# A block gathered three ahead, units of experts in another order, and a last norm with its subtraction on ScalarE

## The chip, the cores and the metric

The kernel runs on one core of a Trainium2 chip. The metric is the time of one execution on the device in microseconds (us). The engines are named as the profile names them: PE is TensorE's matmul side and PEld its weight load, DVE is VectorE, ACT is ScalarE, POOL is GpSimd, SP is SyncE, which issues most DMAs.

## The reference

One decoder block over 512 tokens of width 1024: an adaptive norm, a mixer (a Mamba-2 scan beside a short convolution, joined by gates), a residual and norm, then a mixture of experts, then a residual and norm. Everything is f32. What the change touches is the mixture of experts and the last norm:

```
scores = sigmoid(h @ router_w)             # 512 tokens x 64 experts
e_idx  = top 8 experts of each token, out of its best 4 of 8 groups
gate   = 2.5 * scores[e_idx] / sum(scores[e_idx])
routed[t] = sum over the 8 experts e of t: gate * (silu(h[t] @ w_gate[e]) * (h[t] @ w_up[e])) @ w_down[e]
shared = (silu(h @ sh_gate) * (h @ sh_up)) @ sh_down
x = layer_norm(ALPHA * x + g2 * (routed + shared)) * ln2_g + ln2_b
```

w_gate and w_up are 1024 x 256 and w_down is 256 x 1024 for each expert, so an expert has 3 MiB of weights, read once.

## The kernel before

**Blocks and units.** The experts are ranked by how many tokens they have, and the ranks have fixed capacities (320, 192, 160, 128, 96, 64 and 32 tokens). A block is 128 rows of tokens that belong to one expert or to a few (two of 64, or 96 + 32, or four of 32). Blocks are put together into units of two to six experts by the string ORDER (line 41): each letter is a kind. x is the first rank (3 blocks, 2 experts), y a rank of 192 tokens with a 64 one (2 blocks, 2 experts), z a rank of 160 with a 96 one (2 blocks, 2 experts), f one expert of 128, a a 96 with a 32, p two of 64, q four of 32 (1 block each). So ya has 3 blocks and 4 experts, ap 2 blocks and 4 experts, za 3 and 4, qy 3 and 6, qff 3 and 6, faa 3 and 5. A unit of two experts with fixed names (the static one, 1 block) runs before them. There are 41 blocks in all.

**What happens to a block.** `slots` (line 1108 on) finds its tokens: VectorE compares positions with a ramp (`oh`), TensorE multiplies that one-hot matrix by the tokens' numbers and gates (L1124, tile ps_st), VectorE adds the parts (`red`, L1127), makes an integer list (`idx`, L1129), and GpSimd's queue starts an indirect DMA (L1132) that gathers 128 rows of h from DRAM into one of NXG = 3 buffers `xgs`, used in turn (the profile calls it pg<-h_d,idx). Later `xsteps` transposes the block on TensorE: two halves of four 128x128 transposes (L150, ps_tr<-ident,pg), each half into one of two PSUM banks, from which ScalarE (and for blocks of one expert VectorE, L158 and L160) copies it to `xt`.

**A unit's order on TensorE.** From line 1436 on, for the rest of the units, TensorE's instructions keep the order in which the program is written. In `unit(n)`, TensorE first does the gate and up products of unit n (ps_pj<-...,xt), then, step by step between each other: the transposes of the activations, the combine products of the unit before (L1188 and L1189, which put the weighted rows back to their tokens; VectorE adds them to the residual, L1194), and the transposes of the next unit's blocks by `xs_steps`. That function transposes block i and then calls `need_s(i + NXG)`, which runs `slots` for every block below i + 3. The combine products are used up before the last block of a unit with three blocks is transposed, so its eight transposes stand alone in the order. I call this stretch the transposing stretch. Then come the down products (ps_y<-...,wkr), whose results VectorE weights (L1165) and splits.

**Weights.** SyncE's queue loads the weights in pieces of 1 MiB (lines 869 and 872) into a ring of seven pairs of pages and two more; a piece may be issued up to AHEAD = 10 pieces before its use and when the ring's buffer has been released by the matmuls that read it. An expert has two pieces of gate and up halves and one of down.

**The last norm.** `finish` works on four tiles of 128 tokens. `square` makes the mean and the sum of squares (L1483, ScalarE L1484), `root` the inverse deviation (ScalarE L1488, VectorE L1489), `scale` the result. ENG3 (line 46) says how: for tile 0 ("PP") ScalarE subtracts and scales (L1491, L1492) and GpSimd multiplies by ln2_g (L1501) and adds ln2_b (L1502). For tiles 1 to 3 ("VV") VectorE does it in two instructions with two tensors each (L1497, L1498). Then SyncE writes the tile out (L1503).

Of the kernel before, what the change touches and what calls it, by code (L numbers as in the profile page):

```python
# [8 lines left out]
F32 = mybir.dt.float32  # L9
# [9 lines left out]
T, D, P = 512, 1024, 128  # L19
# [18 lines left out]
NXG = 3  # L38


ORDER = "x qy ya ap za qff ya ap za faa ya ap za faa p"
AHEAD = 10
NDEF = 2
FORD = "q0 r0 s0 q1 r1 s1 q2 r2 s2 q3 r3 s3"
NADA = 3
ENG3 = ("PP", "VV", "VV", "VV")
NWK = 5
AD = "VVVV"
NCV = 4
# [14 lines left out]
def block_kernel(ctx: ExitStack, tc: tile.TileContext, a, out, dbg=None):  # L64
    nc = tc.nc
    dbg = dbg or {}
    V, S, PE, GP, SY = nc.vector, nc.scalar, nc.tensor, nc.gpsimd, nc.sync
# [22 lines left out]
    def bank(tag, bufs, dt=F32):  # L90
        return ps.tile([P, 512], dt, name="ps_" + tag, tag=tag, bufs=bufs)
# [16 lines left out]
    def page(shape, dt=F32, pool=None):  # L108
        n = 1
        for q in shape:  # L110
            n *= q
        assert n == 1024
        if pool or not pw:
            return (pool or pa).tile([P, *shape], dt, name="pg", tag="pg")
        if not halves:
            t = pair([2, 1024], dt)
            halves.extend((t[:, 1], t[:, 0]))
        return halves.pop()
# [618 lines left out]
    rt = ctx.enter_context(tc.tile_pool(name="rt", bufs=1))  # L737
# [159 lines left out]
    def xsteps(src_ap, dst=None, whole=False):  # L897

        hi, lo = dst or [None if whole and i else hold.tile([P, KD, P], F32 if whole else FR, name="xt", tag="hm", bufs=8)
                         for i in range(2)]  # L900
        sv = src_ap.rearrange("p (d k) -> p k d", k=KD)

        def steps():
            for q in range(2):
                tp = bank("tr", 2)
                for k in range(4):
                    transpose(tp[:, k * P:(k + 1) * P], sv[:, 4 * q + k, :])
                tv = tp.rearrange("p (k n) -> p k n", k=4)
                sl_ = slice(4 * q, 4 * q + 4)
                if whole:  # L910
                    S.activation(hi[:, sl_, :], tv, AF.Copy)
                else:
                    split_to(hi[:, sl_, :], lo[:, sl_, :], tv)
                yield

        return (hi, lo), steps()
# [191 lines left out]
    def slots(*parts):  # L1108


        oh = rt.tile([P, NT, P], BF, name="oh", bufs=2)
        w = min(n for _, n, _ in parts)
        i, tiles = 0, []
        for v, n, pays in parts:
            m = len(pays)
            V.tensor_tensor(oh[:, :, i:i + n * m].rearrange("p t (q s) -> p t q s", q=m),
                            iota1[:, None, None, :n].to_broadcast([P, NT, m, n]),
                            v[:, :, :, None].to_broadcast([P, NT, m, n]), op=OP.is_equal)
            i += n * m
            tiles += [p_ for p_ in pays for _ in range(n // w)]  # L1120
        ip = bank("st", 1)
        for t in range(NT):
            for q, p_ in enumerate(tiles):
                PE.matmul(ip[w * q:w * q + w, :6], oh[:, t, w * q:w * q + w], p_[:, t],  # L1124
                          start=(t == 0), stop=(t == NT - 1), tile_position=(0, w * q) if w < P else None)
        red = rt.tile([P, 2], F32, name="red", bufs=8)
        V.tensor_reduce(red, ip[:, :6].rearrange("p (a b) -> p a b", b=3), axis=AX.X, op=OP.add)  # L1127
        idx = rt.tile([P, 1], I32, name="idx", bufs=4)
        V.tensor_scalar(idx, red[:, 0:1], NOTOK, None, op0=OP.add)  # L1129
        xg = xgs[nblk[0] % NXG]  # L1130
        nblk[0] += 1
        GP.indirect_dma_start(out=xg, out_offset=None, in_=h2_d[:, :],  # L1132
                              in_offset=bass.IndirectOffsetOnAxis(ap=idx, axis=0),
                              bounds_check=T - 1, oob_is_err=False)
        return xg, red
# [101 lines left out]
    def static_slots(u):  # L1237
        return slots((pg[:, :, 0, u[0]:u[-1] + 1], P // len(u), [pays[:, :, e, :] for e in u]))
# [61 lines left out]
    def seg(r, n, m=1, v=None):  # L1300
        return (posp if v is None else v)[:, :, r:r + m], n, [pay[:, :, r + i, :] for i in range(m)]

    def second(r):
        pc = rt.tile([P, NT, 1], F32, name="pc")
        V.tensor_scalar(pc, posp[:, :, r:r + 1], 128.0, None, op0=OP.subtract)
        return slots((pc, P, [pay[:, :, r, :]]))
# [20 lines left out]
    for k, n in (("p", 64), ("q", 32)):  # L1327
        m = 128 // n
        for r in of[n][::m]:
            kinds[k].append((tuple(range(r, r + m)),  # L1330
                             [(tuple(range(m)), lambda r=r, n=n, m=m: slots(seg(r, n, m)))]))
    for ks in ORDER.split():

# [18 lines left out]
    def need_s(n):  # L1352
        while len(sl) < min(n, len(allb)):
            sl.append(allb[len(sl)][1]())

    def xs_steps(n):
        while len(xs) < min(n, len(allb)):
            i = len(xs)
            need_s(i + 1)
            r, g = xsteps(sl[i][0], None, len(allb[i][0]) > 1)  # L1360
            xs.append(r)
            yield from g
            need_s(i + NXG)

    def need_x(n):
        drain(xs_steps(n))
# [109 lines left out]
    def finish():  # L1476

        os_, st = {}, {}

        def square(t):  # L1480
            os_[t] = page([D])
            st[t] = const.tile([P, 4], F32, name="fst", bufs=4)
            V.tensor_scalar(st[t][:, 0:1], rsum[:, t, 0:1], rsum[:, t, 1:2], -1.0 / D, op0=OP.add, op1=OP.mult)  # L1483
            S.activation(os_[t], ra[t], AF.Square, bias=st[t][:, 0:1], scale=1.0, accum_out=st[t][:, 1:2])  # L1484

        def root(t):
            nmu, ss, rs, nb = (st[t][:, i:i + 1] for i in range(4))
            S.activation(rs, ss, AF.Sqrt, bias=epsc, scale=1.0 / D)  # L1488
            V.reciprocal(rs, rs)  # L1489
            if ENG3[t] != "VV":  # L1490
                V.tensor_tensor(nb, nmu, rs, op=OP.mult)  # L1491
                S.activation(os_[t], ra[t], AF.Identity, bias=nb, scale=rs)  # L1492

        def scale(t):
            o, nmu, rs = os_[t], st[t][:, 0:1], st[t][:, 2:3]
            if ENG3[t] == "VV":
                V.scalar_tensor_tensor(o, ra[t], nmu, ln2g, op0=OP.add, op1=OP.mult)  # L1497
                V.scalar_tensor_tensor(o, o, rs, ln2b, op0=OP.mult, op1=OP.add)  # L1498
            else:
                e1, e2 = ({"V": V, "P": GP}[e] for e in ENG3[t])  # L1500
                e1.tensor_tensor(o, o, ln2g, op=OP.mult)  # L1501
                e2.tensor_tensor(o, o, ln2b, op=OP.add)  # L1502
            SY.dma_start(out[0, t * P:(t + 1) * P, :], o)  # L1503

        for c in FORD.split():
            {"q": square, "r": root, "s": scale}[c[0]](int(c[1]))
# [35 lines left out]
```

## Time and profile before

| | |
|---|---|
| median of 3 runs | 1628.57 us (1625.51 to 1630.03) |
| the profiled execution | 1629.32 us |
| its span in the trace | 1627.5 us |
| TensorE busy | 1496.8 us, 92% |
| VectorE busy | 974.6 us, 60% |
| ScalarE busy | 645.4 us, 40% |
| GpSimd busy | 230.3 us, 14% |

Times inside the trace count from the start of the span. The 1.8 us by which the execution is longer than its span lie outside the trace. The units of experts run from about 850 to 1600 us, the last norm from 1605 to the end. Idle time of an engine matters only where the next work waits for that engine; the trace gives for each idle stretch what ended it.

### The profile page before, as it was taken

Reading aid. Unit: us, or ns where it says so; the run is one execution under the profiler, and the core shown is the slowest. Engines: PE = TensorE matmul, PEld = TensorE weight load, DVE = VectorE, ACT = ScalarE, POOL = GpSimd, SP = SyncE. Lnnn points to the kernel's source line nnn. Section 1 sums busy time; section 2 is a strip of 40 time slices with the busy share of each in tenths; the row PEclk is TensorE's granted clock in tenths of the full one; section 3 lists DMA queues with packets and bytes.
Section 4 is the critical chain, followed back from the end, with each engine's and each line's share of the span. In section 5 each row is a group of like instructions: output and inputs, shape, how many; then the busy total and the mean of one; then the engine's idle time right before and its main releaser. Section 6 shows DMA issues by size and latency. Waiting matters only on the chain.

```text
span 1627.5 us, 22863 instructions
## 1 busy us (share of the span) xinstructions
PE 1496.8 (92%) x8253; PEld 1018.3 (63%) x8253; DVE 974.6 (60%) x1810; ACT 645.4 (40%) x925; POOL 230.3 (14%) x232
## 2 busy tenths in 40 slices
PE   6999999999999999999978899988889988998893
PEld 3688777787777877887755544545544555554452
DVE  4558778667858556536786535545554554444456
ACT  2456575655634545334542213222341232222222
POOL 0011110111012457300135000000010000000001
PEclk9999999999999999999999999999999999999997
DMA  9653432533441667536227677877988878877671
GB/s 277 170 154 88 113 70 83 147 85 97 117 100 39 203 202 217 167 91 212 108 77 289 234 283 286 305 297 302 386 303 304 309 255 358 317 301 297 253 302 53
DMA packets 194504, 335.67 MB, mean 206 GB/s; under 512 B 13428, under 2 KB 136660, under 8 KB 186196
## 3 DMA queue, kind: packets, MB, share of 16 engines
q1 hardware_dynamic: 183300, 303.73, 53.9%
q0 software_dynamic: 11088, 30.45, 7.3%
q8 instruction: 66, 1.08, 0.3%
q14 instruction: 50, 0.41, 0.1%
HBM read 334.58 MB, written 4.28 MB: 208 GB/s over the span
## 4 chain that ended last, share of the span: by engine, by line
PE 68%; DMA 12%; DVE 8%; issue 6%; ACT 3%; POOL 1%; SPq 1%; DVEq 0%; ACTq 0%; POOLq 0%
PE ps_pj L153 12%; PE ps_pj L154 12%; PE ps_pj L155 12%; PE ps_pj L950 6%; DMA pr<-in_w_up_dram 5%; PE ps_y L950 5%; PE ps_y L1188 4%; PE ps_y L1189 4%; PE ps_tr L150 4%; DMA pg<-h_d,idx 4%; DMA pg<-in_w_ada_dram 2%; DVE wl L160 2%; PE ps_y L153 1%; PE ps_y L155 1%; PE ps_y L154 1%
## 5 line engine op out<-in xcount | busy, mean ns | idle before, releaser
L153 PE MATMUL ps_pj<-hm,wh 128*128 128x512 f32 x680 | 276.3, 407 | 2.0 <-ACT wh L158 2.0
L155 PE MATMUL ps_pj<-hm,wl 128*128 128x512 f32 x680 | 267.4, 394 | 6.2 <-DVE wl L160 6.2
L154 PE MATMUL ps_pj<-hm,wh 128*128 128x512 f32 x680 | 267.4, 393 | 0.0
L160 DVE TENSOR_TENSOR wl<-pg,wh 128x1024 fp32r<-128x1024 f32 (+1 forms) x129 | 157.1, 1224 | 116.9 <-ACT wh L158 116.7
L950 PE MATMUL ps_pj<-pr,xt 128*32 128x512 f32 (+1 forms) x1472 | 212.2, 604 | 9.7 <-DMA pr<-in_w_up_dram 9.7
L158 ACT ACTIVATE wh<-pg 128x1024 fp32r<-128x1024 f32 (+1 forms) x135 | 127.5, 952 | 136.4 <-PE ps_pj L154 104.6
L950 PEld LDWEIGHTS ps_pj<-pr,xt 128*32 128x32 f32 (+1 forms) x1472 | 62.0, 117 | 150.1 <-issue 139.7
L153 PEld LDWEIGHTS ps_pj<-hm,wh 128*128 128x128 f32 x680 | 128.9, 190 | 36.7 <-issue 6.0
L155 PEld LDWEIGHTS ps_pj<-hm,wl 128*128 128x128 f32 x680 | 128.5, 189 | 36.7 <-DVE wl L160 8.8
L154 PEld LDWEIGHTS ps_pj<-hm,wh 128*128 128x128 f32 x680 | 128.5, 189 | 28.9 <-issue 3.4
L160 DVE TENSOR_TENSOR wl<-pr,wh 128x1024 fp32r<-128x1024 f32 x72 | 86.9, 1220 | 96.6 <-ACT wh L158 96.0
L1132 POOL DMA_INDIRECT pg<-h_d,idx x41 | 48.1, 1174 | 597.2 <-PE ps_y L1189 163.6
L1194 DVE TENSOR_TENSOR res<-res,ps_y 128x512 f32<-128x512 f32 x120 | 82.2, 686 | 75.3 <-PE ps_y L1189 73.7
L150 PE MATMUL ps_tr<-ident,pg 128*128 128x128 f32 x392 | 71.1, 314 | 49.0 <-DMA pg<-h_d,idx 45.7
L158 ACT ACTIVATE wh<-pr 128x1024 fp32r<-128x1024 f32 x72 | 74.8, 1054 | 101.5 <-DMA pr<-in_w_up_dram 67.4
L950 PE MATMUL ps_y<-pr,wkr 128*32 128x512 f32 (+1 forms) x736 | 106.1, 618 | 0.8 <-DVE wk L1165 0.8
L150 PEld LDWEIGHTS ps_tr<-ident,pg 128*128 128x128 f32 x392 | 58.9, 196 | 60.5 <-issue 32.6
L1165 DVE SCALAR_TENSOR_TENSOR wk<-ps_y,red,pg 128x512 f32<-128x512 f32 x82 | 61.0, 748 | 35.3 <-PE ps_y L155 20.1
L366 POOL TENSOR_TENSOR pg<-pg 128x1024 f32<-128x1024 f32 x28 | 74.1, 2665 | 54.6 <-ACT pg L364 54.5
L927 ACT ACTIVATE sg<-ps_pj 128x256 f32<-128x256 f32 x44 | 16.8, 384 | 159.7 <-PE ps_pj L950 99.2
L153 PE MATMUL ps_pj<-pg,wh 128*128 128x512 f32 x192 | 76.0, 396 | 1.3 <-ACT zs L431 1.2
L155 PE MATMUL ps_pj<-pg,wl 128*128 128x512 f32 x192 | 76.3, 397 | 0.0
(394 smaller groups left out, 2648.8 us busy)
## 6 DMA issues: line engine op xcount, KB each, us to landing
pr<-in_w_gate_dram SPq DMA_DIRECT2D x128, 512.0 KB, 9.8
pr<-in_w_up_dram SPq DMA_DIRECT2D x128, 512.0 KB, 10.1
pr<-in_w_down_dram SPq DMA_DIRECT2D x64, 1024.0 KB, 11.7
pg<-in_w_in_dram SPq DMA_DIRECT2D x88, 512.0 KB, 4.9
pg<-in_w_ada_dram SPq DMA_DIRECT2D x48, 512.0 KB, 5.9
bc<-acs_d POOLq DMA_DIRECT2D x32, 256.0 KB, 4.5
pg<-in_w_ssd_out_dram SPq DMA_DIRECT2D x16, 512.0 KB, 4.5
pg<-in_w_sc_out_dram SPq DMA_DIRECT2D x8, 512.0 KB, 4.0
```

The costliest lines, as they stand in the source:

```text
L150: return PE.transpose(o, i, ident[:n, :n])
L153: PE.matmul(o, lh, rh, start=start, stop=False)
L154: PE.matmul(o, lh, rl, start=False, stop=False)
L155: PE.matmul(o, ll, rh, start=False, stop=stop)
L158: S.activation(hi, src, AF.Copy)
L160: V.tensor_tensor(lo, src, rw(hi), op=OP.subtract)
L366: GP.tensor_tensor(part[i], part[i], w, op=OP.add)
L950: PE.matmul(o[w * i:w * i + w, :], x[:, w * i:w * i + w], m, start=start, stop=stop, tile_position=(0, w * i))
L1165: V.scalar_tensor_tensor(yg, o, red[:, 1:2], g2b[:, ns_], op0=OP.mult, op1=OP.mult)
L1188: PE.matmul(o, oh_, yh[:, ns_], start=(i == 0), stop=False)
L1189: PE.matmul(o, oh_, yl[:, ns_], start=False, stop=(i == len(ps_) - 1))
L1194: V.tensor_tensor(ra[t][:, ns_], ra[t][:, ns_], o, op=OP.add)
```

## The change

The string ORDER has the same units in another order: the two units of six experts, second and sixth before, are now third and seventh, and the others are placed anew around them. `xs_steps` asks for one block more: after block i has been transposed, `slots` runs for every block below i + 4, so the gather of block i + 3 starts as soon as its buffer, that of block i, is free. `red`, which a block needs until its down products, has ten buffers instead of eight. In the last norm tiles 1 to 3 go the way of tile 0, with VectorE in GpSimd's place: ScalarE subtracts the mean and scales, VectorE multiplies by ln2_g and adds ln2_b.

```diff
-ORDER = "x qy ya ap za qff ya ap za faa ya ap za faa p"
+ORDER = "x ya qy za ap ya qff za ya ap faa za ap faa p"
-ENG3 = ("PP", "VV", "VV", "VV")
+ENG3 = ("PP", "AVV", "AVV", "AVV")
...
-        red = rt.tile([P, 2], F32, name="red", bufs=8)
+        red = rt.tile([P, 2], F32, name="red", bufs=10)
...
             xs.append(r)
             yield from g
-            need_s(i + NXG)
+            need_s(i + 1 + NXG)
...
             else:
-                e1, e2 = ({"V": V, "P": GP}[e] for e in ENG3[t])
+                e1, e2 = ({"V": V, "P": GP}[e] for e in ENG3[t][-2:])
                 e1.tensor_tensor(o, o, ln2g, op=OP.mult)
                 e2.tensor_tensor(o, o, ln2b, op=OP.add)
```

What moves on TensorE, in the stretch that transposes the blocks of unit qff. Before, during unit za: the first rows transpose block one of qff, then a one-hot product (ps_st_8840) whose list fills buffer pg_6527, and the last two rows are the transposes of block three out of that same buffer.

```order
L150 MATMUL ps_tr_8826<-ident_95,pg_6525 128x128 x4
...
L1124 MATMUL ps_st_8840<-pay_5885,oh_8838 128x6
...
L150 MATMUL ps_tr_8867<-ident_95,pg_6526 128x128 x4
L1124 LDWEIGHTS oh_8874
L1124 MATMUL ps_st_8876<-pay_5885,oh_8874 128x6
...
L150 MATMUL ps_tr_8890<-ident_95,pg_6527 128x128 x4
L150 MATMUL ps_tr_8897<-ident_95,pg_6527 128x128 x4
```

In the change, the one-hot product for block three of qff (ps_st_8979) stands one unit earlier, behind the transposes of the last block of the unit before, and the stretch that transposes qff's blocks comes after that unit's down products:

```order
L150 MATMUL ps_tr_8965<-ident_95,pg_6527 128x128 x4
L150 MATMUL ps_tr_8971<-ident_95,pg_6527 128x128 x4
L1124 LDWEIGHTS oh_8977
L1124 MATMUL ps_st_8979<-pay_5885,oh_8977 128x6
...
L950 MATMUL ps_y_9002<-pr_8642,wkr_8853 32x512 x3
...
L150 MATMUL ps_tr_9287<-ident_95,pg_6526 128x128 x4
...
L150 MATMUL ps_tr_9323<-ident_95,pg_6527 128x128 x4
L150 MATMUL ps_tr_9330<-ident_95,pg_6527 128x128 x4
```

The one-hot product of a unit's third block has moved from the middle of the stretch that transposes it to the end of the stretch before. The rows on GpSimd's queue are the same gathers in the same buffers. The matmuls of one kind are as many as before.

The second place is the last norm on VectorE (fst is the small tile of statistics, pr the pages with the results and with ln2_g and ln2_b, res the residual). Before:

```order
L1497 SCALAR_TENSOR_TENSOR pr_12550<-res1_73,fst_12561,pr_12547 128x1024
L1489 RECIPROCAL fst_12551<-fst_12551 128x1
L1489 RECIPROCAL fst_12561<-fst_12561 128x1
L1491 TENSOR_TENSOR fst_12551<-fst_12551 128x1
L1498 SCALAR_TENSOR_TENSOR pr_12550<-pr_12550,fst_12561,pr_12547 128x1024
L1497 SCALAR_TENSOR_TENSOR pr_12569<-res2_74,fst_12570,pr_12547 128x1024
L1497 SCALAR_TENSOR_TENSOR pr_12569<-res3_75,fst_12578,pr_12547 128x1024
L1489 RECIPROCAL fst_12570<-fst_12570 128x1
L1489 RECIPROCAL fst_12578<-fst_12578 128x1
L1498 SCALAR_TENSOR_TENSOR pr_12569<-pr_12569,fst_12570,pr_12547 128x1024
L1498 SCALAR_TENSOR_TENSOR pr_12569<-pr_12569,fst_12578,pr_12547 128x1024
```

In the change:

```order
L1491 TENSOR_TENSOR fst_12561<-fst_12561 128x1
L1501 TENSOR_TENSOR pr_12550<-pr_12550,pr_12547 128x1024
L1489 RECIPROCAL fst_12572<-fst_12572 128x1
L1502 TENSOR_TENSOR pr_12550<-pr_12550,pr_12547 128x1024
L1491 TENSOR_TENSOR fst_12572<-fst_12572 128x1
L1489 RECIPROCAL fst_12582<-fst_12582 128x1
L1491 TENSOR_TENSOR fst_12582<-fst_12582 128x1
L1501 TENSOR_TENSOR pr_12571<-pr_12571,pr_12547 128x1024 x2
L1502 TENSOR_TENSOR pr_12571<-pr_12571,pr_12547 128x1024 x2
```

The six large instructions of tiles 1 to 3 are six others, and the small L1491 of tiles 2 and 3 now stand behind the two large instructions of tile 1. On ScalarE, whose rows follow, three activations of 128x1024 are new, and the squares of tile 3 stand behind those of tiles 0 and 1:

```order
L1484 ACTIVATE pr_12571,fst_12572<-res2_74,fst_12572 128x1024
L1492 ACTIVATE pr_12550<-res0_72,fst_12551 128x1024
L1492 ACTIVATE pr_12550<-res1_73,fst_12561 128x1024
L1488 ACTIVATE fst_12572<-fst_12572,epsc_103 128x1
L1484 ACTIVATE pr_12571,fst_12582<-res3_75,fst_12582 128x1024
L1488 ACTIVATE fst_12582<-fst_12582,epsc_103 128x1
L1492 ACTIVATE pr_12571<-res2_74,fst_12572 128x1024
L1492 ACTIVATE pr_12571<-res3_75,fst_12582 128x1024
```

Before, the four squares (L1484) stood ahead of the one L1492; the activations of tiles 2 and 3 now stand last.

## Rows read from the trace of the kernel before

**Rows 1.** The page's first part: busy time of TensorE, its share of the span, instructions.

```profile
PE 1496.8 (92%) x8253; PEld 1018.3 (63%) x8253; DVE 974.6 (60%) x1810; ACT 645.4 (40%) x925; POOL 230.3 (14%) x232
```

**Rows 2.** Who waited for whom, TensorE alone, from 880 to 1600 us: the waiting instruction, the one waited for, us in total, times, longest.

```profile
PE ps_tr L150 <- DMA pg<-h_d,idx: 45.7, 12, 5.4
PE ps_pj L950 <- DMA pr<-in_w_up_dram: 9.7, 8, 1.6
```

**Rows 3.** TensorE's timeline: start, us, instruction, count, and in brackets the idle time before it and what ended it. The first two of the twelve transposes that waited for a gather, and three of the other ten.

```profile
893.24 1.13 PE L150 MATMUL ps_tr<-ident,pg 128*128 128x128 f32 x8 [2.00 <-DMA pg<-h_d,idx]
899.65 0.95 PE L150 MATMUL ps_tr<-ident,pg 128*128 128x128 f32 x4 [1.90 <-DMA pg<-h_d,idx]
...
1128.56 1.94 PE L150 MATMUL ps_tr<-ident,pg 128*128 128x128 f32 x8 [4.16 <-DMA pg<-h_d,idx]
...
1186.04 1.50 PE L150 MATMUL ps_tr<-ident,pg 128*128 128x128 f32 x8 [3.88 <-DMA pg<-h_d,idx]
...
1279.91 1.13 PE L150 MATMUL ps_tr<-ident,pg 128*128 128x128 f32 x8 [2.15 <-DMA pg<-h_d,idx]
```

**Rows 4.** The gathers' line, L1132: time from issue to landing of all 41.

```profile
DMA to landing us min/median/max: 3.6/4.4/11.2
```

**Rows 5.** GpSimd's timeline: the gather for which the transposes at 1128.56 waited.

```profile
1124.23 0.99 POOL L1132 DMA_INDIRECT pg<-h_d,idx  x1 [34.86 <-PE ps_y L1189]
```

**Rows 6.** ScalarE's and VectorE's timeline just before and in that wait: the copy of the half transposed before, and the last of VectorE's queue.

```profile
1124.36 0.60 ACT L158 ACTIVATE xt<-ps_tr 128x512 fp32r<-128x512 f32 x1 [0.78 <-PE ps_tr L150]
1124.99 0.69 DVE L160 TENSOR_TENSOR xt<-ps_tr,xt 128x512 fp32r<-128x512 f32 x1
...
1127.52 0.21 DVE L1160 TENSOR_SCALAR tok<-red 128x1 f32<-128x1 f32 x2
```

**Rows 7.** Stretches of 8 us from the start of each of the ten later transposes that waited: length, busy us of each engine with its instructions, the granted clock (PEclk), DMA share, GB/s.

```profile
933.80:941.80 8.00, 8.00 (x39) 6.62 (x40) 3.79 (x9) 2.53 (x5) 0.99 (x1) 0.79 0.40 120
991.80:999.80 8.00, 7.96 (x54) 3.80 (x54) 4.28 (x11) 2.77 (x4) 1.99 (x2) 0.79 0.41 120
1084.80:1092.80 8.00, 8.00 (x54) 3.59 (x56) 4.29 (x12) 2.45 (x4) 0.99 (x1) 0.82 0.26 70
1128.60:1136.60 8.00, 8.00 (x52) 5.26 (x56) 4.94 (x11) 2.46 (x4) 0.99 (x1) 0.79 0.24 74
1186.00:1194.00 8.00, 7.96 (x55) 3.79 (x56) 5.16 (x10) 3.31 (x5) 2.10 (x2) 0.79 0.35 94
1279.90:1287.90 8.00, 7.99 (x72) 2.97 (x72) 6.30 (x15) 2.85 (x5) 2.24 (x2) 1.00 0.40 128
1323.90:1331.90 8.00, 7.96 (x40) 5.82 (x44) 2.55 (x7) 2.80 (x5) 0.99 (x1) 0.62 0.28 89
1378.90:1386.90 8.00, 7.96 (x40) 5.69 (x44) 2.75 (x7) 3.00 (x5) 0.99 (x1) 0.64 0.28 85
1471.60:1479.60 8.00, 7.95 (x60) 3.10 (x62) 3.89 (x12) 1.82 (x3) 0.99 (x1) 0.68 0.33 96
1517.90:1525.90 8.00, 8.00 (x48) 5.24 (x52) 3.32 (x5) 3.31 (x5) 0.00 (x0) 0.80 0.03 9
```

**Rows 8.** The same view of four other stretches: nearly all units; one wait for a gather; a stretch of gate and up products; a transposing stretch in which the next unit has two blocks (unit ya, ahead of ap).

```profile
880.00:1584.00 704.00, 639.98 (x4071) 351.07 (x4071) 358.78 (x656) 198.96 (x313) 47.04 (x40) 0.96 0.80 301
1125.00:1128.50 3.50, 0.00 (x0) 0.00 (x0) 2.73 (x10) 0.00 (x0) 1.80 (x2) 1.00 0.53 170
1206.00:1226.00 20.00, 20.00 (x124) 10.05 (x121) 8.01 (x10) 5.94 (x9) 0.00 (x0) 1.00 1.02 414
1230.00:1240.00 10.00, 10.00 (x70) 6.88 (x70) 7.89 (x21) 3.06 (x5) 2.11 (x2) 1.00 0.51 180
```

**Rows 9.** TensorE's timeline: gate and up products that waited for weights, in units qy (the first two) and qff.

```profile
965.64 1.02 PE L950 MATMUL ps_pj<-pr,xt 128*32 128x512 f32 x2 [1.56 <-DMA pr<-in_w_up_dram]
968.08 2.74 PE L950 MATMUL ps_pj<-pr,xt 128*32 128x512 f32 x12 [1.42 <-DMA pr<-in_w_up_dram]
...
1161.47 1.04 PE L950 MATMUL ps_pj<-pr,xt 128*32 128x512 f32 x2 [1.60 <-DMA pr<-in_w_up_dram]
1164.10 1.49 PE L950 MATMUL ps_pj<-pr,xt 128*32 128x512 f32 x11 [1.58 <-DMA pr<-in_w_up_dram]
```

**Rows 10.** The last norm in the timeline of ScalarE, VectorE and GpSimd: the first square, the one L1492, GpSimd's two instructions and the last four of VectorE's large ones (two merged in a row).

```profile
1605.79 1.15 ACT L1484 ACTIVATE pr<-res,fst 128x1024 f32<-128x1024 f32 x1 [6.71 <-DVE fst L1483]
...
1610.70 1.23 ACT L1492 ACTIVATE pr<-res,fst 128x1024 f32<-128x1024 f32 x1
1610.88 4.56 DVE L1497 SCALAR_TENSOR_TENSOR pr<-res,fst,pr 128x1024 f32<-128x1024 f32 x2
...
1612.01 2.34 POOL L1501 TENSOR_TENSOR pr<-pr 128x1024 f32<-128x1024 f32 x1 [95.95 <-ACT pr L1492]
1614.43 3.20 POOL L1502 TENSOR_TENSOR pr<-pr 128x1024 f32<-128x1024 f32 x1
...
1615.54 4.36 DVE L1498 SCALAR_TENSOR_TENSOR pr<-pr,fst 128x1024 f32<-128x1024 f32 x2
```

**Rows 11.** VectorE and GpSimd earlier in the trace, each with an instruction of two 128x1024 tensors: one of VectorE's beside one of GpSimd's, and one with GpSimd idle.

```profile
604.35 2.38 POOL L366 TENSOR_TENSOR pg<-pg 128x1024 f32<-128x1024 f32 x1 [1.27 <-ACT pg L364]
605.25 2.56 DVE L160 TENSOR_TENSOR wl<-pg,wh 128x1024 fp32r<-128x1024 f32 x1 [6.65 <-ACT wh L158]
...
609.54 1.23 DVE L160 TENSOR_TENSOR wl<-pg,wh 128x1024 fp32r<-128x1024 f32 x1 [1.12 <-ACT wh L158]
```

## The prediction

> **What bounds the kernel now.** I read the busy times first: TensorE is busy for 92% of the span [rows 1], so a gain must come from its idle time or its clock. The table of waits of TensorE over the units says what its idle time is: 45.7 us in 12 waits of the transposes for a gather, and 9.7 us for weights; the rest is small [rows 2]. TensorE's timeline shows where the twelve are: two at the start (2.00 and 1.90 us, blocks of unit x, while the static unit runs), and ten in the transposing stretches, each in front of the eight transposes of a unit's third block [rows 3]. One of them step by step: the one-hot product for the third block comes only after the first block has been transposed, the gather is issued at 1124.23 [rows 5], TensorE runs out of other work at 1124.4 (4.16 us ahead of the transposes), the data lands about 4.4 us after issue [rows 4], and the transposes start at 1128.56 after 4.16 us of idling. Units whose next unit has two blocks have no such wait: TensorE is busy for 10.00 of 10 us there [rows 8]. So the ten waits are what a gather issued too late costs: 45.7 - 2.0 - 1.9 = 41.8 us.
>
> They cost more than their length. In the 8 us after nine of the ten waits the granted clock is below 1 (0.62 to 0.82), while TensorE is busy for nearly all of those 8 us [rows 7]. The lower of the two levels is 1.2 GHz, half of 2.4, so the time lost there is 8 x (1 - clock): 1.68 + 1.68 + 1.44 + 1.68 + 1.68 + 0 + 3.04 + 2.88 + 2.56 + 1.60 = 18.2 us. The one that left the clock at 1.00 had the shortest idle time ahead of it, 2.15 us [rows 3].
>
> **The change part by part.**
>
> *Gather one block earlier.* The number of gathers, one-hot products and transposes stays. With i + 4 the gather of a unit's third block is issued behind the transposes of the last unit's third block, so it has a whole unit to land, some 40 us, against 11.2 us for the slowest gather now [rows 4]. Its buffer is freed by the transposes just before, so it waits for nothing else; GpSimd's queue has only gathers there. Of the 41.8 + 18.2 = 60.0 us I take all away.
>
> What is late next: the eight transposes use two banks, and their second half must wait until the bank of the second block has been copied and split: 0.60 on ScalarE and 0.69 on VectorE [rows 6], 1.29 us, against about 0.6 us that the first half of the eight takes by itself (half of 1.13 [rows 3]). So 0.7 us of each wait stays, 10 x 0.7 = **7 us back**. From below it is nothing, as in the stretch of [rows 8] with two blocks; from above it is VectorE's queue, which in the wait at 1125 runs on until 1127.7 [rows 6], 3.3 us after TensorE stopped. I take the price near the lower end because only the copy stands in the way of the transposes; the rest of VectorE's queue makes lists and masks for later. Ten `red` instead of eight only lengthen the life of a small tile: nothing, and without them the gathers' lists would wait for the down products.
>
> *The two waits at the start.* Unit x's third gather is issued one step earlier, but the DMA engines are full of weights then, and its transposes also stand earlier in TensorE's order, among the static unit's down products. I take no gain; bounds are a gain of 3.9 (both waits [rows 3]) and a loss of 2.5.
>
> *The order of units.* No matmul is added. What can move are the waits for weights. Unit qy, behind x, waits 1.56 + 1.42 = 2.98 us; qff, behind a unit of four experts that holds four down pieces of the ring, waits 1.60 + 1.58 = 3.18 us [rows 9]. Both six-expert units now stand behind a unit of four, which makes 0.2 us; the ap units, behind ya so far, stand behind za twice. I take **+1 us**, with bounds of -6 (both units' waits go) and +8 (five units, the two of six and the three ap, wait longer by 1.6, the longest single wait).
>
> *The last norm.* Now the first square starts at 1605.79, the one L1492 at 1610.70, and VectorE ends at 1615.54 + 4.36 = 1619.90 [rows 10]. VectorE's large instructions cost about 1.2 us by themselves, but beside GpSimd's they go one after the other with them: 2.56 against 1.23 us [rows 11], and two pairs of 4.56 and 4.36 us here. After the change VectorE has no large instruction less, and ScalarE has three of 1.23 us more. In the new order one square (1.15) less stands ahead of L1492 of tile 0, which runs from 1609.6 to 1610.8, and that of tile 1 to 1612.0. GpSimd multiplies from 1610.8 to 1613.1, VectorE's multiplication of tile 1 then takes until 1614.3, GpSimd's addition until 1616.5, VectorE's addition until 1617.7. Only then comes the small L1491 of tile 2, for which ScalarE's L1492 waits: 1617.8 to 1619.1 and, for tile 3, 1620.3. Four large instructions of VectorE follow from 1619.1 on: 1624.0. That is **4.1 us later**. If VectorE and GpSimd did not get in each other's way, VectorE's pair of tile 1 would end at 1614.5, and the rest, by the same steps, at 1620.9: 1 us later. I take 4.1, since the row beside GpSimd in [rows 11] and the two pairs in [rows 10] show them one after the other. The end of the norm is the end of the program, so this is on the path in full.
>
> *Sum*: -41.8 - 18.2 + 7 + 4.1 + 1 = -47.9. The profiled execution took 1629.32, which gives 1581.4; it stands 0.75 above the median of 1628.57, so I predict **1581 us**.
>
> **The rivals.**
>
> *The stream of weights takes the waits' place.* All of the units carry 704 us x 301 GB/s = 212 MB [rows 8]; at 414 GB/s that is 512 us, so there is room on the whole. But in a wait the DMA engines still work, with a share of 0.53 over 3.5 us [rows 8], 1.9 us of transfers each. If these then stand in front of the weights of the next gate and up products, ten times 1.9 us return, and with idle times of that length half of the 18.2 us of clock: 28 us, so 1609. Against it: the first pieces of the next unit are in the ring by then, the later ones start only when the down products release pages, and between the two the DMA share falls to between 0.03 and 0.41 [rows 7].
>
> *The stream holds the two units of six experts alone.* Such a unit moves six times 3 MiB of weights and three gathers of 0.5 MiB, 20.4 MB, and qff takes 57.5 us from one transposing stretch to the next [rows 3], so it runs at 355 GB/s. If the stream could go no faster over a whole unit, each of the two units would keep its wait and its share of the clock, 5 to 6 us, with all other terms as above, and the time would be 1592. Against it: the gate and up products take weights at 414 GB/s over 20 us, with TensorE busy throughout [rows 8]; at that rate 20.4 MB take 49.3 us, less than the 51.6 that remain when 5.9 us go. The Trainium skill, "DMA: Bandwidth & Descriptors", Specifications, puts HBM's limit for one core at about 358 GB/s, which would make this rival the forecast: 57 us for such a unit, and a sum of about -37 instead of -47.9. The trace does not agree, with its 414 GB/s.
>
> *VectorE takes the waits' place (slower than before).* The one-hot product behind the eight transposes needs a mask (L1116) that stands in VectorE's queue among the work that now fills the wait. TensorE would stop there instead, in the same ten places. The price is the wait that stays in each: at 3.3 us and with the clock still falling, 33 + 18.2 + 5.1 - 60.0 = -4, about the same; from 3.7 us each on the change is slower, and at 4.2, the wait of today, it is 1628.6 + 5 = 1634. For it: VectorE is busy for 2.73 of 3.5 us in the wait [rows 8]. Against it: the stretch with two blocks has VectorE busy for 7.89 of 10 us and TensorE never stops.
>
> *The change does not do what it says.* If something else held the gather back (its list, or GpSimd's turn), the waits would stay and only the norm's 4.1 and the order's 1 us would show: 1634. Against it is the order of the one-hot product, a unit earlier.
>
> **How the numbers follow.** My forecast has 0.78, with its own range from 1566 (no wait left, norm 1 us, weights a little better) to 1598 (2 us of each wait left, weights worse). The stream of weights has 0.11, the stream in two units 0.03, VectorE 0.05, no effect 0.03. The range of 1564 to 1608 takes in the forecast's own, the time of 1592, and the lighter half of the stream's. About 0.3%, 5 us, is what a measurement of this kernel can tell from no change. Faster: 0.78 + 0.11 + 0.03 = 0.92; the others at 1625 to 1634 I split into 0.03 the same and 0.05 slower.
>
> **What would show it.** Right: no waits of the transposes for gathers in the ten places; a granted clock near 1 in the 8 us behind them; gathers issued about 40 us ahead of their transposes; VectorE's last large instruction 18 us after the first square instead of 14. Wrong: waits for weights (L950, L153) well above 9.7 us would be the stream's rival; waits of L1124 or L150 for VectorE or ScalarE above 2 us each would be VectorE's; an end of the norm as early as before would mean that VectorE and GpSimd overlap.

## The result and the profile after

The changed kernel takes 1590.22 us (median; 1586.00 to 1595.45) against 1629.30 for the kernel before beside it: a ratio of 0.9763 [0.9726, 0.9799], 39 us faster, with 1581 forecast and 1564 to 1608 as the range. The profiled execution took 1591.21 us with a span of 1589.4.

TensorE's busy share and, from 860 to 1600 us, who it waited for (columns as in [rows 2]):

```profile
PE 1490.2 (94%) x8253; PEld 1015.0 (64%) x8253; DVE 974.9 (61%) x1813; ACT 648.4 (41%) x928; POOL 227.3 (14%) x232
```

```profile
PE ps_pj L950 <- DMA pr<-in_w_up_dram: 10.7, 9, 2.0
PE ps_pj L154 <- DVE wl L160: 5.5, 6, 1.8
PE ps_pj L153 <- ACT wh L158: 4.6, 4, 1.6
PE ps_y L154 <- DVE wl L160: 1.6, 1, 1.6
...
PE ps_tr L150 <- ACT xt L911: 1.5, 2, 0.8
...
PE ps_tr L150 <- DMA pg<-h_d,idx: 0.9, 2, 0.8
...
PE ps_tr L150 <- DVE xt L160: 0.6, 1, 0.6
```

The 45.7 us of waits for gathers [rows 2] are down to 0.9. The waits for weights (the first four rows; wh and wl are the split halves of a weight page) add up to 22.4 us; the same rows of the kernel before add up to 15.4 (9.7 in [rows 2], 4.8 and 0.9).

A gather and the transposes that it feeds, for block three of qff, the place of [rows 5] and of the 4.16 us in [rows 3]. GpSimd's and TensorE's timelines:

```profile
1121.92 0.99 POOL L1132 DMA_INDIRECT pg<-h_d,idx  x1 [0.30 <-issue]
```

```profile
1157.35 0.71 PE L150 MATMUL ps_tr<-ident,pg 128*128 128x128 f32 x4
1158.64 0.71 PE L150 MATMUL ps_tr<-ident,pg 128*128 128x128 f32 x4 [0.58 <-DVE xt L160]
```

It is issued 35 us ahead of its transposes. The second half of them waits 0.58 us for the copy of its bank, and in most units it waits for nothing. In the 8 us from the start of the third blocks' transposes [rows 7] the clock is now 1.00 in nine of the ten places and 0.98 in the other.

The stretch from the second half of the static block's transposes to the first L1483, with the columns of [rows 8]: first before, then after.

```profile
876.60:1605.50 728.90, 661.60 (x4154) 363.24 (x4154) 375.61 (x692) 202.67 (x319) 47.71 (x42) 0.96 0.78 293
```

```profile
878.90:1564.00 685.10, 651.56 (x4154) 357.70 (x4154) 375.35 (x692) 202.06 (x319) 44.71 (x42) 0.99 0.82 311
```

It is 43.8 us shorter. Idle time (length less busy time) went from 67.3 to 33.5. The clock's loss, summed over pieces of 4 us as 4 x (1 - clock), went from 25.6 to 10.2. That is 33.8 + 15.4 = 49.2, so 5.4 us came back as busy time (busy time less the clock's loss: 636.0 before, 641.4 after), with as many matmuls as before. What precedes the stretch took 2.3 us more, and what follows it, the last norm, 3.4 us more.

The last norm on ScalarE, VectorE and GpSimd, for comparison with [rows 10]:

```profile
1564.29 1.15 ACT L1484 ACTIVATE pr<-res,fst 128x1024 f32<-128x1024 f32 x1 [6.73 <-DVE fst L1483]
...
1568.07 2.35 ACT L1492 ACTIVATE pr<-res,fst 128x1024 f32<-128x1024 f32 x2
```

```profile
1570.46 2.35 DVE L1501 TENSOR_TENSOR pr<-pr 128x1024 f32<-128x1024 f32 x1 [2.95 <-ACT pr L1492]
1572.84 3.25 DVE L1502 TENSOR_TENSOR pr<-pr 128x1024 f32<-128x1024 f32 x1
1576.01 0.15 DVE L1491 TENSOR_TENSOR fst<-fst 128x1 f32<-128x1 f32 x1
...
1577.46 2.36 DVE L1501 TENSOR_TENSOR pr<-pr 128x1024 f32<-128x1024 f32 x2 [1.04 <-ACT pr L1492]
1579.74 2.35 DVE L1502 TENSOR_TENSOR pr<-pr 128x1024 f32<-128x1024 f32 x2
```

```profile
1569.38 2.35 POOL L1501 TENSOR_TENSOR pr<-pr 128x1024 f32<-128x1024 f32 x1 [89.19 <-ACT pr L1492]
1571.80 3.20 POOL L1502 TENSOR_TENSOR pr<-pr 128x1024 f32<-128x1024 f32 x1
```

VectorE's last large instruction ends at 1579.74 + 2.35 = 1582.09, 17.8 us after the first square; before it was 14.1. Beside GpSimd, VectorE's two take 2.35 and 3.25 us; alone, a pair takes 2.36.

### The profile page after: what moved, and what is told of

It is laid out like the page before. It is cut to its first block, busy times and chain, and to the rows that moved or that the text cites. A ratio compares the mean times of both kernels' runs of the same rounds, so it can differ in the third digit from the quotient of the medians.

```text
span 1589.4 us, 22875 instructions
## 1 busy us (share of the span) xinstructions
PE 1490.2 (94%) x8253; PEld 1015.0 (64%) x8253; DVE 974.9 (61%) x1813; ACT 648.4 (41%) x928; POOL 227.3 (14%) x232
## 4 chain that ended last, share of the span: by engine, by line
PE 71%; DMA 13%; DVE 8%; ACT 3%; issue 2%; POOL 1%; SPq 1%; DVEq 0%; ACTq 0%; POOLq 0%
PE ps_pj L153 12%; PE ps_pj L154 12%; PE ps_pj L155 12%; DMA pr<-in_w_up_dram 8%; PE ps_pj L950 7%; PE ps_y L950 5%; PE ps_y L1188 5%; PE ps_y L1189 5%; PE ps_tr L150 4%; DMA pg<-in_w_ada_dram 2%; DVE wl L160 2%; PE ps_y L153 1%; POOL pg L366 1%; PE ps_y L483 1%; PE ps_y L155 1%
## 5 line engine op out<-in xcount | busy, mean ns | idle before, releaser
L1132 POOL DMA_INDIRECT pg<-h_d,idx x41 | 45.2, 1102 | 562.0 <-DVE oht L1161 175.1
L950 PE MATMUL ps_y<-pr,wkr 128*32 128x512 f32 (+1 forms) x736 | 102.7, 596 | 1.3 <-DVE wk L1165 1.3
L928 DVE TENSOR_TENSOR sg<-sg,ps_pj 128x256 f32<-128x256 f32 x44 | 18.4, 420 | 110.3 <-ACT sg L927 110.3
L153 PE MATMUL ps_pj<-pg,wh 128*128 128x512 f32 x192 | 76.0, 396 | 1.4 <-ACT zs L431 1.4
L154 PE MATMUL ps_pj<-pg,wh 128*128 128x512 f32 x192 | 75.7, 395 | 0.0
L416 DVE SCALAR_TENSOR_TENSOR wk<-ps_pj,cw,wk 128x511 f32<-128x511 f32 (+2 forms) x93 | 68.3, 742 | 7.4 <-ACT wk L414 7.0
## 6 DMA issues: line engine op xcount, KB each, us to landing
pr<-in_w_up_dram SPq DMA_DIRECT2D x128, 512.0 KB, 10.2
```

The lines of the kernel that those rows point to most:

```text
L153: PE.matmul(o, lh, rh, start=start, stop=False)
L154: PE.matmul(o, lh, rl, start=False, stop=False)
L416: V.scalar_tensor_tensor(acc[:, s:], o[:, :T - s], cw[:, 3 - s, tl:tl + 1], acc[:, s:], op0=OP.mult, op1=OP.add)
L950: PE.matmul(o[w * i:w * i + w, :], x[:, w * i:w * i + w], m, start=start, stop=stop, tile_position=(0, w * i))
```

## The experiments

**One part at a time.** The first question: is the gain all the gather's, and do the 7 us of new waits for weights come from the order of units, or from the stream of weights as soon as the gathers are early?

```diff
-        red = rt.tile([P, 2], F32, name="red", bufs=8)
+        red = rt.tile([P, 2], F32, name="red", bufs=10)
-            need_s(i + NXG)
+            need_s(i + 1 + NXG)
```

> The kernel before with the earlier gathers alone (and ten buffers for the sums); its order of units and its last norm stay as they were. My theory: nearly all of the gain is here. The waits on gathers between 880 and 1600 us fall from 45.7 us to about 2, the clock next to them comes back, and the last norm stays 14 us from the first square to the last large instruction. If the weight waits that the changed kernel shows (about 22 us of pauses of 0.4 us and more and some 8 us of lowered clock behind them, against about 15 and 3) come from the new order of the units, this kernel has them as before, about 15 us, and its time is 1572 to 1580 us. The rival: the stream of weights is what fills in once the gathers are early, whatever the order; then the weight waits here are 20 us or more and the time is 1583 to 1590 us.

Measured: 1573.87 us, ratio 0.9643 [0.9602, 0.9684]: 58 us faster, and so faster than the whole change. TensorE's waits for weights, and the stretch from the static block to the last norm:

```profile
PE ps_pj L950 <- DMA pr<-in_w_up_dram: 9.7, 9, 1.6
PE ps_pj L154 <- DVE wl L160: 5.2, 6, 1.6
...
PE ps_pj L153 <- ACT wh L158: 0.3, 1, 0.3
```

```profile
871.00:1541.60 670.60, 643.78 (x4154) 353.10 (x4154) 374.10 (x694) 201.12 (x319) 44.31 (x42) 1.00 0.84 319
```

No row for gathers is left, the clock is 1.00, and the weights are waited for as long as before, 15.2 us. The rival of the stream falls: in the old order early gathers call up no new waits for weights.

The order alone, on the kernel before:

```diff
-ORDER = "x qy ya ap za qff ya ap za faa ya ap za faa p"
+ORDER = "x ya qy za ap ya qff za ya ap faa za ap faa p"
```

> The kernel before with the new order of units alone. If the order makes the weight waits of the changed kernel, this kernel is slower than the kernel before by 5 to 12 us (1634 to 1641), with 20 us or more of pauses on weights, unless the gather waits, which stay at 40 to 50 us, hide them by giving the transfers time. If the stream makes them once the gathers are early, this kernel takes 1625 to 1632 us, as before, with pauses on weights of about 15 us.

Measured: 1637.64 us, 1.0017 [0.9989, 1.0044], about 3 us slower, which can't be told from no change.

```profile
PE ps_tr L150 <- DMA pg<-h_d,idx: 43.0, 13, 5.3
PE ps_pj L950 <- DMA pr<-in_w_up_dram: 10.0, 9, 2.2
PE ps_pj L154 <- DVE wl L160: 6.2, 8, 1.8
PE ps_pj L153 <- ACT wh L158: 3.8, 4, 1.4
```

The waits for weights take 20.0 us here, 4.6 more than before, with no gather made earlier, so the order makes these waits; 2.7 us are made up for at the gathers.

The last norm alone, on the kernel before:

```diff
-ENG3 = ("PP", "VV", "VV", "VV")
+ENG3 = ("PP", "AVV", "AVV", "AVV")
```

> The kernel before with the changed last norm alone. My theory: the last large instruction of VectorE ends 17.5 to 18.5 us after the first square and no longer 14.1, and the whole takes 3.4 to 4.1 us more, 1632 to 1633.5. The rival, that the outgoing transfers or something else hide the end of the norm: 1629, as before.

Measured: 1632.76 us, 0.9997 [0.9970, 1.0025]: 3.4 us lie within that interval, so the time doesn't tell. The trace does (ScalarE's first square, VectorE's last pair):

```profile
1605.58 1.15 ACT L1484 ACTIVATE pr<-res,fst 128x1024 f32<-128x1024 f32 x1 [6.71 <-DVE fst L1483]
```

```profile
1621.03 2.35 DVE L1502 TENSOR_TENSOR pr<-pr 128x1024 f32<-128x1024 f32 x2
```

1623.38 - 1605.58 = 17.8 us, against 14.1.

The changed kernel with the old norm, that is gathers and order:

```diff
-ENG3 = ("PP", "AVV", "AVV", "AVV")
+ENG3 = ("PP", "VV", "VV", "VV")
```

> The changed kernel with the last norm of the kernel before: earlier gathers and new order. My theory: 3.4 to 4.1 us less than the changed kernel, 1586 to 1587, all of it after the first square; the stretch ahead as in the changed kernel (685 us from the second transposes of the static block to the first square). The rival, that the norm costs nothing: 1590.

Measured: 1579.96 us, 0.9680 [0.9641, 0.9719]; 6.1 us above the gathers alone on the same chip. From the first L1483 to the end it takes 21.8 us (25.4 in the changed kernel), as expected. But the stretch ahead took 678.4 us, not 685, with the same instructions. So 7 us of the profiled execution of the changed kernel lie between two executions of the same instructions; in it the clock lost 10.2 us in that stretch, here 5.1.

**The parts together.** The changed kernel once more, and beside it the changed kernel with the old order.

> The changed kernel once more, beside its two neighbours on one chip. My theory by now: three terms add up. Earlier gathers alone gave a ratio of 0.9643, the new order on top of them 0.0037 more, and the last norm takes 3.1 to 3.6 us more from the first square to the end: 0.970 to 0.972, so 52 to 47 us less than the kernel before on the same chip. If the ratio of 0.976 measured first stands instead, something that the runs apart don't show costs another 6 to 10 us when the parts are together.

Measured: 1587.21 us, 0.9731 [0.9691, 0.9771]: 44 us less than before, between what the parts add up to and the first result.

```diff
-ORDER = "x ya qy za ap ya qff za ya ap faa za ap faa p"
+ORDER = "x qy ya ap za qff ya ap za faa ya ap za faa p"
```

> The changed kernel with the order of units of the kernel before: earlier gathers and new norm. My theory: the new order costs 6 to 8 us of waits for weights, so this takes 6 to 8 us less than the changed kernel on the same chip, with pauses on weights as in the kernel with the earlier gathers alone (16 us in the units, against about 22). The rival, that the order costs nothing and the difference seen so far was one between executions: the same time as the changed kernel, within 3 us.

Measured: 1579.60 us, 0.9685 [0.9644, 0.9726], 7.6 us less than the changed kernel beside it. Its waits for weights are 15.0 us, those of the other 20.1. The new order costs 6 to 8 us, measured twice: here no execution of the one kernel is as fast as the slowest of the other, while the 6.1 us above lie between executions that overlap.

**Where the order costs.** Both orders have qy and qff waiting for weights (pauses of 0.4 us and more): 2.98 and 5.2 us in the kernel before, 3.0 and 4.4 with the gathers alone, 3.9 and 5.5 in the changed kernel. Most of the difference is at ap and faa. In the old order ap, za, faa follow each other; in the new one ap stands right ahead of faa, twice. In the changed kernel the two pairs wait 1.41 + 3.67 + 2.04 + 2.18 = 9.3 us for weights; with the gathers alone the second and third ap and the two faa wait 4.0. So this one move was put into the kernel with the gathers alone:

```diff
-ORDER = "x qy ya ap za qff ya ap za faa ya ap za faa p"
+ORDER = "x qy ya ap za qff ya za ap faa ya za ap faa p"
```

> The kernel with the earlier gathers alone, with its two units of five experts (faa) moved behind a unit with two blocks (ap), as in the changed kernel's order, and no longer behind one with three (za); the units of six stand where the kernel before has them. My theory of the order's cost: a unit ap has as many weights as za and fewer matmuls, so behind it the ring of weights has less of a lead, and faa then waits: 3 to 4 us on weights in each of the two units faa (1.7 and 0.8 us with za ahead), and the time is 3 to 6 us above that of the earlier gathers alone. The rival, that the place of the six-expert units makes the waits: the units faa wait 2 us or less each, and the time is that of the earlier gathers alone.

Measured: 1582.80 us, 0.9709 [0.9668, 0.9750], which is 7 to 9 us above the two medians of the gathers alone (1573.87, and 1575.56 below), more than the 3 to 6 expected, with intervals of the ratios that overlap. TensorE in the first unit faa, in this kernel:

```profile
1318.98 2.35 PE L950 MATMUL ps_pj<-pr,xt 128*32 128x512 f32 x20 [1.50 <-DMA pr<-in_w_up_dram]
1323.99 0.49 PE L153 MATMUL ps_pj<-wh,xt 128*128 128x512 f32 x1 [1.42 <-ACT wh L158]
1325.25 0.50 PE L154 MATMUL ps_pj<-wl,xt 128*128 128x512 f32 x1 [0.76 <-DVE wl L160]
```

3.68 us, and 2.18 in the second; in the kernel with the old order that was run beside it, 0.76 in each:

```profile
1321.72 0.50 PE L154 MATMUL ps_pj<-wl,xt 128*128 128x512 f32 x1 [0.76 <-DVE wl L160]
```

The two units ap add 1.29 and 1.79. Together 8.9 us, about as in the changed kernel. The stretch from the static block to the last norm:

```profile
878.30:1551.60 673.30, 642.15 (x4154) 353.16 (x4154) 374.54 (x694) 201.25 (x319) 45.53 (x42) 1.00 0.84 317
```

TensorE's idle time in it is 31.2 us, against 26.8 with the gathers alone, and the stretch is 2.7 us longer, so the waits are shown in the trace, and the 7 to 9 us only by the medians. The second faa waits less than the 3 us expected.

An account of why ap, in units qff, ap and faa with the gathers alone (columns as in [rows 8], from one transposing stretch to the next):

```profile
1094.40:1145.70 51.30, 45.66 (x289) 27.27 (x288) 30.82 (x53) 17.72 (x26) 3.03 (x3) 1.00 0.92 349
1194.10:1233.70 39.60, 37.99 (x251) 19.13 (x250) 16.84 (x34) 7.71 (x14) 1.98 (x2) 1.00 0.78 294
1275.90:1323.20 47.30, 45.30 (x329) 24.66 (x328) 26.64 (x48) 15.32 (x24) 3.34 (x3) 1.00 0.93 349
```

In qff and faa the DMA engines are taken up to 0.92 and more, at 349 GB/s. What a unit needs, worked out from its 3 MiB per expert and 0.5 MiB per block over its length: qff 398 GB/s, faa 366, ap 344, za (41.9 us) 338, ya (48.8 us) 290. By this estimate a unit above 349 lives on the lead that the ring has built up, and ap, at 344, builds up next to none.

The traces bear this out in part only. The rate of 349 is no limit: the first unit faa of the kernel with the move carries 362 GB/s, the unit ya behind it 369.

```profile
1286.90:1333.30 46.40, 42.72 (x304) 22.70 (x303) 25.19 (x46) 13.88 (x22) 3.48 (x3) 1.00 0.94 362
1333.30:1377.90 44.60, 44.33 (x306) 24.46 (x305) 26.77 (x48) 15.45 (x24) 2.96 (x3) 1.00 0.96 369
```

In ap the engines move only 294, at a share of 0.78. And ap and za together need the same in either order. The lead can be counted from the DMA packets in the trace: the MiB of weights moved by the time of a unit's first gate and up product, beyond those of the units before it. The two units faa start with 4.25 and 4.58 MiB in this kernel, and with 4.70 and 4.69 in the one with the old order beside it. The 0.45 and 0.11 MiB less are 1.4 and 0.3 us at 349 GB/s, while the waits grew by 2.9 and 1.4. So the lead is smaller behind ap, but it explains less than half of the waits; the rest is open.

**The norm's price.** The changed kernel without GpSimd in the norm:

```diff
-ENG3 = ("PP", "AVV", "AVV", "AVV")
+ENG3 = ("AVV", "AVV", "AVV", "AVV")
```

> The changed kernel with GpSimd taken out of the last norm: VectorE multiplies and adds for the first tile too. My theory: VectorE's and GpSimd's large instructions go one after the other when they run at the same time, so handing GpSimd's two to VectorE costs nothing: VectorE's eight large instructions take 1.2 us each, and the last ends 16 to 16.5 us after the first square, against 17.8 in the changed kernel. The rival, that the two engines work side by side and VectorE's instructions are 2.3 us long by themselves when ScalarE is busy: 20 us or more.

Measured: 1584.38 us in one execution. VectorE:

```profile
1564.50 2.36 DVE L1501 TENSOR_TENSOR pr<-pr 128x1024 f32<-128x1024 f32 x2 [1.82 <-ACT pr L1492]
1566.78 2.35 DVE L1502 TENSOR_TENSOR pr<-pr 128x1024 f32<-128x1024 f32 x2
...
1570.70 2.36 DVE L1501 TENSOR_TENSOR pr<-pr 128x1024 f32<-128x1024 f32 x2 [1.24 <-ACT pr L1492]
1572.98 2.35 DVE L1502 TENSOR_TENSOR pr<-pr 128x1024 f32<-128x1024 f32 x2
```

The first square starts at 1559.46, so the norm takes 15.9 us. VectorE does two instructions more and is done 1.9 us earlier.

Squares and roots of all tiles first, in the changed kernel:

```diff
-FORD = "q0 r0 s0 q1 r1 s1 q2 r2 s2 q3 r3 s3"
+FORD = "q0 q1 q2 q3 r0 r1 r2 r3 s0 s1 s2 s3"
```

> The changed kernel with the squares and roots of the last norm ahead of all scaling. My step for the changed norm said that the small product that ScalarE's scaling of tile 2 waits for stands behind tile 1's two large instructions on VectorE. If that wait (4.1 us of ScalarE) costs time, ScalarE scales all four tiles without a pause here, and the last large instruction ends 16.5 to 17 us after the first square, against 17.8. The rival, that VectorE's large instructions beside GpSimd's set the end alone: 17.8 or more.

Measured: 1590.32 us in one execution. ScalarE, then VectorE:

```profile
1563.92 1.15 ACT L1484 ACTIVATE pr<-res,fst 128x1024 f32<-128x1024 f32 x1 [6.73 <-DVE fst L1483]
...
1569.20 4.62 ACT L1492 ACTIVATE pr<-res,fst 128x1024 f32<-128x1024 f32 x4
```

```profile
1571.59 5.63 DVE L1501 TENSOR_TENSOR pr<-pr 128x1024 f32<-128x1024 f32 x2 [1.82 <-ACT pr L1492]
...
1580.66 1.23 DVE L1502 TENSOR_TENSOR pr<-pr 128x1024 f32<-128x1024 f32 x1
```

ScalarE scales four tiles without a pause, and the end is at 18.0 us all the same. The rival was right: the 4.1 us for which ScalarE waits in the changed kernel cost nothing by themselves. Here VectorE's first multiplications, beside GpSimd's two instructions, take 5.63 us for two.

**A version that beats both.** The gathers alone, with VectorE doing all of the norm in the old way, and the gathers alone once more beside it:

```diff
-ENG3 = ("PP", "VV", "VV", "VV")
+ENG3 = ("VV", "VV", "VV", "VV")
```

> The kernel with the earlier gathers alone, with GpSimd and ScalarE's scaling taken out of its last norm: VectorE does both steps of all four tiles, as the kernel before does for three. If the mutual hindrance of VectorE and GpSimd is what the norm pays for, VectorE's eight large instructions take 1.28 us each, as two of them did in the kernel before while GpSimd was idle, and the last ends 11.5 to 12.5 us after the first square, against 14.1 in the kernel before: 1.5 to 2.5 us less than the kernel with the earlier gathers alone on the same chip, so 1570 to 1575. The rival, that GpSimd's help is worth its price: 14 us or more.

> The kernel with the earlier gathers alone once more, on the chip of the run with VectorE alone in the norm: a ratio of 0.964 to 0.968 to the kernel before, 52 to 59 us less, and no waits of the transposes for gathers in the ten places.

Measured: 1574.58 us, 0.9640 [0.9614, 0.9665], beside 1575.56, 0.9656 [0.9627, 0.9685]: 59 and 56 us less than before. The norm on ScalarE (first square) and VectorE:

```profile
1553.29 1.15 ACT L1484 ACTIVATE pr<-res,fst 128x1024 f32<-128x1024 f32 x1 [7.44 <-DVE fst L1483]
```

```profile
1554.56 2.48 DVE L1497 SCALAR_TENSOR_TENSOR pr<-res,fst,pr 128x1024 f32<-128x1024 f32 x2 [0.94 <-ACT pr L1484]
1557.15 2.48 DVE L1498 SCALAR_TENSOR_TENSOR pr<-pr,fst 128x1024 f32<-128x1024 f32 x2
1559.62 1.27 DVE L1497 SCALAR_TENSOR_TENSOR pr<-res,fst,pr 128x1024 f32<-128x1024 f32 x1
1560.88 1.27 DVE L1497 SCALAR_TENSOR_TENSOR pr<-res,fst,pr 128x1024 f32<-128x1024 f32 x1
1562.06 2.48 DVE L1498 SCALAR_TENSOR_TENSOR pr<-pr,fst 128x1024 f32<-128x1024 f32 x2
```

11.25 us from the first square to the last large instruction, 2.9 less than before, a little under the 11.5 expected. From L1483 to the end of the span it is 19.0 against 21.4 us; the 1.0 us between the medians is within their spread. Both are 11 us and more ahead of the changed kernel.

## Why the prediction was right, and where its sizes were off

The time lies in the range and the likeliest case is the one that came: the waits go and nothing takes their place one for one. Term by term:

| term | forecast | measured |
|---|---|---|
| ten waits and their clock, less what the banks keep | -60.0 + 7 | -56 and -58 (with the start) |
| two waits at the start | 0 (-3.9 to +2.5) | about -3.6 |
| order of units | +1 (-6 to +8) | +6.1 and +7.6 |
| last norm | +4.1 (or +1) | +3.7 to its last large instruction, +3.4 to the end |

**The gathers.** The mechanism holds in each point: no wait for a gather in the ten places, the gather shown 35 us ahead, the clock at 0.98 to 1.00 behind those places. The clock gave back more than the 18.2 us forecast: in the stretch it lost 25.6 us before, and 1.7 and 4.8 in two executions with the gathers alone. The term for the banks was too large. I had 0.7 us left in each of ten places; with the gathers alone the transposes in those places wait 0.62 + 0.69 us in one of them, 0.55 and 0.24 in two and not at all in the rest, 2.1 us. The step put all of ScalarE's and VectorE's copy (1.29 us) behind the first half's transposes; in most places the bank was free by then. That the sum for the gathers came out so close is in part luck: 5 us less stayed at the banks and 3 to 6 us more clock came back, and 5 to 6 us of busy time, which the step did not have, took much of that away again.

**The start.** I took no gain. From the static block's transposes to the first ones of the unit behind x it is 47.25 us before (876.62 to 923.87) and 43.6 with the gathers alone (870.98 to 914.59): nearly both waits of [rows 3] went. The DMA engines were as full there as I took them to be, with a share of 1.00 from 880 to 892 us in the kernel with the gathers alone, and the gathers landed in time all the same.

**The order.** This is the step that failed in size, and the reason given for it was wrong. I looked at the two units of six experts alone and let their waits shrink because a unit of four stands ahead of them. They didn't shrink. Counted as above, qff starts with 4.6 MiB of weights ahead in either order; it stood behind a unit of four, za, before as well. And qy lost by the move: it starts with 6.0 MiB behind x, a unit of two experts, and with 4.6 behind ya. Most of the cost came at the pairs ap, faa, which the prediction named (the ap units "behind za twice") but did not follow to the unit behind. Its upper bound of +8, five units that wait 1.6 us longer, came near, though two of the units that wait longer, the two faa, are not among its five.

**The norm.** The 4.1 us are 3.7, and the cause, VectorE and GpSimd one after the other, is the one forecast: with GpSimd out of it the same work, and more on VectorE, is done earlier, twice. The Trainium skill, "SBUF — State Buffer", section "SBUF: two separate sides", has the pair of ports of these two engines as an exclusive lock, held for the whole instruction, which also covers an instruction of VectorE with two inputs in SBUF; the rows agree (2.36 us for two alone, 2.35 and 3.25 for one beside GpSimd). The part of the step about the small L1491 was wrong: it waits where I said, but its wait was not what set the end.

**The rivals.** The stream of weights did not take the waits' place: 15.2 us of waits for weights with early gathers, 15.4 without. VectorE did not either: in the ten places no wait for it or for ScalarE is longer than 0.7 us with the gathers alone, or than 0.84 in the changed kernel (L1124 for the mask, L1116, as that rival has it, in one place). The stream in the two six-expert units gives about the measured time, 1592, but not by its mechanism, since neither unit kept its wait for a gather. What I held against it was weak, though: 414 GB/s over 20 us [rows 8] is not the rate of a whole unit, which in qff and faa was 349 GB/s with the DMA engines taken up to 0.92 and 0.93. The Trainium skill's figure of about 358 GB/s ("DMA: Bandwidth & Descriptors", Specifications) is near that rate of a whole unit; the 369 of a unit ya and the 414 of a shorter stretch are above it.

**What stays open.** The parts add up to -57 + 7 + 3.4 = -47 us. The changed kernel measured -39 [-45, -33] and -44 [-50, -37], and I can't say whether the 3 to 8 us left are an effect of the parts together or of chips and executions. The norm's 3.4 us are those of the trace. Its medians, of runs at different times, differ by 5.7 us in the old order (1579.60 against 1573.87), by 7.2 in the new (1587.21 against 1579.96) and by nothing on the kernel before; with the first two the parts come to about -44. Executions of one kernel differ by up to 15 us (1565.3 at a mean clock of 0.987, 1580.3 at 0.979, with the gathers alone). Part of that lies ahead of the units: the stretch from the static block on starts at 870.7, 878.9 and 879.9 us in three profiled executions whose kernels differ in nothing but the last norm. The changed kernel's two profiled executions lost 10.2 and 6.9 us of clock in the units, those with the gathers alone 1.7 and 4.8. Nor is it settled why 5 to 6 us of the idle time taken away came back as busy time of TensorE; it did so with the gathers alone too (643.8 us busy with 1.7 of clock lost, against 661.6 with 25.6).

## What to carry to other kernels

When a wait is taken away, look at the resource that it gave time to: here the DMA engines went from 0.78 to 0.84 of the stretch with the gathers alone, and no new wait came of it. Before units change places, count what the ring holds when each of them starts (6.0 MiB behind x, 4.6 behind ya), and not the experts of the unit ahead; the order made new waits for weights with late gathers as well as with early ones (4.6 us, and 5 to 7). Try the parts of a change apart: one of three carried more than the whole gain, and the two others gave back some 10 us of it. And don't share elementwise work on two-input tiles between VectorE and GpSimd at the end of a kernel before a trace has shown that they run side by side.

## What the runs showed that I had not expected

- Handing GpSimd's two instructions to VectorE made the norm shorter in both forms: 17.8 to 15.9 us, and 14.1 to 11.25 us where VectorE took over ScalarE's scaling as well. Beside GpSimd, VectorE's instructions with two tensors took 2.3 to 3.3 us each instead of 1.2.
- Over the whole units qff and faa the stream of weights gave 349 GB/s with DMA shares of 0.92 and 0.93, though it gave 414 over 20 us, and 369 over a unit ya at a share of 0.96.
- Small pauses for weights can cost the clock too: in the changed kernel the clock was 0.57 in the 4 us from 1380, behind pauses of 1.49, 1.42 and 0.76 us, while the kernel with the gathers alone, with pauses of up to 1.65 us, went through its units at 1.00 until 6 us before the last norm. The 10.2 us that the clock lost in the changed kernel's stretch were lost in six dips to the lower level, five of them right behind waits for weights.
